# A decoder layer on eight cores: the second half's out projection from a bf16 copy of its weights, its normalisation with factors in PSUM, and four smaller moves around them

## The chip, the cores and the metric

The kernel runs on all 8 cores of one Trainium2 chip: two dies, cores 0 to 3 and 4 to 7. Each core does its own share of the tokens, and the time is the device time of the slowest core in microseconds (us). PE is the matmul engine, DVE the vector engine, ACT the scalar engine, POOL (GpSimd) the fourth compute engine, and SP an engine that does nothing here but issue DMAs. SBUF and PSUM are on-chip memories; PSUM is what matmuls write to, used here as 8 banks.

Some executions of these 8-core versions show a lower clock and the time is some per cent longer (3459.4 us once for the kernel before). Only fast runs are compared here. A profile names source lines of its own kernel, so one operation has another line number before and after; the text gives both.

## The reference, cut to what matters

One layer: a projection, two kinds of attention, an RMS norm for each group of heads, the out projection, a LayerNorm, a SwiGLU feed-forward block, a second LayerNorm.

```python
y = jnp.concatenate([rms_norm(ya, g_mix_a), rms_norm(yb, g_mix_b)], axis=-1)   # (tokens, 2048)
mix = jnp.einsum('bse,ed->bsd', y, w_out)                                      # out projection
x = layer_norm(ALPHA * x + mix, ln1_g, ln1_b)
x = layer_norm(ALPHA * x + swiglu(x, w_up, w_down), ln2_g, ln2_b)
```

The change touches the end of the attention, the RMS norm of y, the out projection and the sums of the first LayerNorm.

## The kernel before

A core has 2048 tokens. The out projection is made in two halves of 1024 tokens (`st` 0 and 1). A half has 32 tiles, one for each block `n` of 128 output columns and each group `hh` of 512 tokens. In the first half the first six tiles are half done early, while attention ends. For a tile, PE does 16 matmuls into one PSUM bank, DVE makes z = alpha * x + bank (which frees the bank and one of four x buffers), ACT squares z, and GpSimd adds z and its square to running sums. SP loads x.

```python
for si, (n, hh) in enumerate(steps):
    bk = OUT_BK[si % 6] if st == 0 else si % 4      # 6 banks in the first half, 4 in the second
    load_xr(si + 3)                                 # x of the third tile from here, on SP
    if st == 0 and si < 8:                          # the second half's y, 2 loads per tile, on SP
        for c in (KCB + KCA[:7])[2 * si:2 * si + 2]:
            k.y_load(1, c)
    ...                                             # out_mm: the matmuls of the tile
    if hh == 1:
        wdone(k, ("o", st, n))                      # frees the weights' slot and issues the next load
    for _ in range(2):                              # first half: normalise the second half's y
        if st == 0 and si >= 8 and k.norms:
            out_norm(k, *k.norms.pop(0))
    if si >= 1 and fins:
        fins.pop(0)()                               # LayerNorm sums of the half before, on PE
    ...                                             # DVE: z = alpha * x + bank
    ...                                             # stats(): ACT squares z, GpSimd sums z and z*z
    # ... then LayerNorm tiles of the half before, if due
```

The weights of a block `n` (512 KB in bf16) go through a ring of five slots. The loads cast from float32 and are issued by GpSimd, in the same queue of instructions as GpSimd's sums:

```python
def wfill(k):
    while k.wlist:
        key, src, n, a, p = k.wlist[0]
        if any(lo < p + n * 2 and p < hi for (_, lo, hi) in k.wlive):
            return
        ...
        if key[:2] == ("d", 1):
            k.S.dma("sp", v, src, [k.bwdb[key[2]]], [b], "ws")
        else:
            k.S.dma("pool", v, src, [], [b], "ws")

def out_norm(k, st, c, hh):          # y = y * gain * factor, on DVE, two inputs in SBUF
    r, br = k.rs[st * 2 + hh + (0 if c >= 8 else 4)]
    ...
    k.S.dve(lambda: nc.vector.scalar_tensor_tensor(out=v, in0=v, scalar=k.gmix[:, c:c + 1], in1=r, ...), [b, br, k.bsmall], [b])

def rs_load(k, rsum):                # the factors, on ACT's queue
    for t in range(4):
        k.S.dma("act", k.rs[t][0], k.rb_d[:, t * 512:(t + 1) * 512], [rsum[t]], [k.rs[t][1]], "rs")
```

Waits between engines are semaphores that the kernel's helper derives from what each operation reads and writes. In the traces an engine takes its instructions in order, and one that waits holds back all behind it; that includes the issue of a DMA.

The softmax here doesn't subtract the row's maximum and nothing guards it: scores larger than these inputs give would overflow.

## Time and profile before

Median 3056.03 us in the first three runs (3055.99 to 3057.72). The profiled execution was a further one, of 3060.24 us. Its page, taken on the slowest core (7): busy time of each engine with its share of the span, and the shares of the chain of waits that ended last.

```profile
PE 2987.2 (98%) x15999; PEld 1427.6 (47%) x15999; DVE 1063.9 (35%) x1442; ACT 656.1 (21%) x906; POOL 624.0 (20%) x591
...
PE 87%; DMA 5%; DVE 3%; issue 2%; ACT 2%; POOL 1%; ACTq 0%; SPq 0%; DVEq 0%; POOLq 0%
```

PE is busy 98% of the span. What is left to win by moving other work is in the gaps between matmuls, and in the clock: after or within four of PE's stops on this core the clock records show 0.5 for 3.4 to 10.2 us, and in these stretches a matmul of 128x512 starts every 427 ns, at full clock every 216 (medians). The groups of instructions show whose gaps those are. Columns: line, engine, operation, output<-input, shapes and count; busy us and mean ns of one; idle time of the engine just before them, with what ended it. L1135 is the out projection, L1375 the up projection after it, L1124 `out_norm`.

```profile
L1375 PE MATMUL sp<-arena 128*128 128x512 bf16 x5632 | 1219.0, 380 | 10.2 <-DVE arena L1271 10.2
...
L1135 PE MATMUL sp<-arena 128*128 128x512 bf16 x1024 | 233.3, 391 | 3.0 <-DVE arena L1271 2.3 <-DVE arena L1124 0.6
...
L1124 DVE SCALAR_TENSOR_TENSOR arena<-arena 128x512 bf16<-128x512 bf16 x64 | 76.6, 1237 | 4.3 <-ACT arena L966 4.3
```

The out projection hardly waits (3.0 us). The up projection waits once, 10.2 us, for L1271, which makes z. The waits of SP's queue say why these z are late: the last x loads reuse z slots, and SP stands until the stores of x1 out of these slots have landed (waited for: us in total, times, longest).

```profile
SPq L183 <- DMA x1s<-arena: 28.3, 4, 13.7
```

Stages are compared by windows. Columns: window, its length, busy us of PE, PEld (weight load), DVE, ACT and POOL with counts, granted clock, share of DMA time in use, GB/s. The first two windows are the first half of the out projection, 1060 to 1180 the second, 1180 to 1225 the start of the up projection.

```profile
968.00:1020.00 52.00, 51.93 (x235) 23.12 (x234) 31.57 (x29) 7.69 (x13) 37.09 (x32) 0.97 0.92 203
1020.00:1060.00 40.00, 37.67 (x174) 16.45 (x172) 33.72 (x29) 7.22 (x12) 34.66 (x30) 1.00 0.78 146
1060.00:1125.00 65.00, 61.83 (x255) 26.88 (x254) 36.22 (x55) 27.93 (x42) 46.66 (x45) 0.91 0.91 176
1125.00:1180.00 55.00, 55.00 (x234) 23.87 (x233) 30.53 (x47) 21.11 (x30) 36.32 (x33) 0.91 0.96 219
1180.00:1225.00 45.00, 34.81 (x151) 15.14 (x150) 4.76 (x7) 6.87 (x10) 16.97 (x16) 0.89 0.67 127
```

PE loses 10 of 45 us in 1180 to 1225. DMA is near full in the second half. Last, the timeline of the attention's tail. Columns: start, duration, engine, line, operation, output<-input, count, and in brackets the idle time before and what ended it.

```profile
893.22 2.15 ACTq L127 DMA_DIRECT2D arena<-rb  x4
...
895.47 0.60 ACT L925 ACTIVATE arena<-sp 128x512 f32<-128x512 f32 x1 [3.44 <-issue]
...
897.73 0.61 PE L897 MATMUL sp<-arena 128*128 128x128 bf16 x8 [1.95 <-DVE arena L928]
...
908.03 0.75 DVE L331 SCALAR_TENSOR_TENSOR arena<-sp,arena 128x512 f32<-128x512 f32 x1
...
908.89 1.02 DVE L334 TENSOR_TENSOR arena<-arena 128x512 bf16<-128x512 f32 x1
...
910.65 0.82 PE L908 MATMUL sp<-arena 128*128 128x64 bf16 x17 [2.14 <-DVE arena L700]
```

ACT issues the four factor loads for 2.15 us, so the activation behind them starts after 3.44 us of idle, and PE stops for 1.95 us. Later two operations of the rope (the rotation of queries and keys by position) stand on DVE ahead of a mask (L700), and PE stops for 2.14 us.

**A bookkeeping of stops.** I summed, from the trace, the gaps in which no matmul runs and half of the time at clock 0.5 (cold clock, in what follows), by stretch. I call the sum the loss. Not every stop has cold clock after it: the one near 700 was 1.92 us long on all 8 cores before, and 3.4 us at 0.5 followed it on cores 3, 4, 6 and 7 alone. A gap and a stretch of cold clock count where they begin. Where the clock is already at 0.5 while PE still stands, both are counted, so the loss runs somewhat high: without this overlap the whole of 640 to 1225 is 40.7 before. Where a reading turns on it, the text says so. The mean of the 8 cores for the kernel before, in us: 3.6 in 690 to 720, 13.7 in 880 to 943 (the tail), 2.3 in 968 to 1020, 2.1 in 1020 to 1060, 4.7 in 1060 to 1125, 8.2 in 1125 to 1225; with the little between them, 42.1 in 640 to 1225. Time lost at a third clock, 0.81, is kept apart (0.1875 of its length, for the records have 0.8125 there, and matmuls of 128x512 start every 263 ns; 6.8 us here).

### The profile page before, as it was taken

The numbers are of one execution on the slowest core, as the hardware profiler recorded it, in microseconds if no ns is written. First come the engines' busy times: TensorE is split into PE (matmuls) and PEld (weight loads), VectorE is DVE, ScalarE is ACT, GpSimd is POOL, SyncE is SP. The second block draws the span as 40 slices with busy tenths as digits, with TensorE's granted clock in tenths as the row PEclk, the third lists the DMA queues.
The fourth block names the chain that finished last, engine by engine and source line by source line (L and its number), as shares of the span: only waits on it lengthen the run. The fifth ranks groups of instructions, "written<-read, shape, count | busy, mean of one in ns | idle before, by whom it ended". The sixth has DMA issues, their size and how long they took to land.

```text
span 3059.1 us, 40208 instructions; the slowest of 8 cores (3041.8 to 3059.1 us)
## 1 busy us (share of the span) xinstructions
PE 2987.2 (98%) x15999; PEld 1427.6 (47%) x15999; DVE 1063.9 (35%) x1442; ACT 656.1 (21%) x906; POOL 624.0 (20%) x591
## 2 busy tenths in 40 slices
PE   8999999999999998999999999999999999999997
PEld 3445554556664443444444444444444444444443
DVE  1655546887785862430000100000222100000142
ACT  0000002765654142320000001111222000011222
POOL 2000001553444864000000002222000000002233
PEclk9999999999999998999999999999999999999998
DMA  9961213245668898564434348889666434434574
GB/s 166 183 146 54 83 48 76 56 120 136 150 148 176 163 179 175 127 129 75 80 72 83 70 95 204 206 206 200 144 153 137 86 71 82 72 109 180 177 234 149
DMA packets 192956, 397.92 MB, mean 130 GB/s; under 512 B 88961, under 2 KB 106625, under 8 KB 171778
## 3 DMA queue, kind: packets, MB, share of 16 engines
q0 software_dynamic: 31296, 167.06, 32.7%
q1 hardware_dynamic: 144194, 196.81, 21.6%
q10 hardware_dynamic: 17280, 31.46, 2.9%
q8 instruction: 129, 2.11, 0.3%
q14 instruction: 57, 0.47, 0.1%
HBM read 470.52 MB, written 91.82 MB: 184 GB/s over the span
## 4 chain that ended last, share of the span: by engine, by line
PE 87%; DMA 5%; DVE 3%; issue 2%; ACT 2%; POOL 1%; ACTq 0%; SPq 0%; DVEq 0%; POOLq 0%
PE sp L1375 40%; PE sp L1408 20%; PE sp L487 7%; PE sp L474 6%; PE sp L737 5%; DMA arena<-xres 3%; DMA arena<-wv 1%; PE sp L555 1%; DVE arena L1124 1%; PE sp L908 1%; DMA x1s<-arena 1%; PE sp L1135 1%; DVE arena L928 1%; PE sp L796 1%; ACT arena L926 1%
## 5 line engine op out<-in xcount | busy, mean ns | idle before, releaser
L1375 PE MATMUL sp<-arena 128*128 128x512 bf16 x5632 | 1219.0, 380 | 10.2 <-DVE arena L1271 10.2
L1375 PEld LDWEIGHTS sp<-arena 128*128 128x128 bf16 x5632 | 551.6, 98 | 678.1 <-issue 16.2
L1408 PE MATMUL sp<-arena 128*128 128x512 bf16 x2816 | 608.3, 379 | 0.0
L1383 DVE TENSOR_TENSOR arena<-sp,arena 128x512 bf16<-128x512 f32 x176 | 121.8, 692 | 998.6 <-ACT arena L1382 998.6
L1408 PEld LDWEIGHTS sp<-arena 128*128 128x128 bf16 x2816 | 275.5, 98 | 332.6 <-issue 0.6
L1382 ACT ACTIVATE arena<-sp 128x512 f32<-128x512 f32 x176 | 105.2, 598 | 903.8 <-PE sp L1375 903.8
L127 POOL DMA_DIRECT2D arena<-wup x88 | 46.8, 532 | 1086.0 <-PE sp L1375 1069.9
L1175 POOL TENSOR_TENSOR arena<-arena 128x512 f32<-128x512 f32 x119 | 156.1, 1312 | 458.3 <-DVE arena L1419 404.8
L1135 PE MATMUL sp<-arena 128*128 128x512 bf16 x1024 | 233.3, 391 | 3.0 <-DVE arena L1271 2.3
L737 PE MATMUL sp<-arena 128*128 128x512 bf16 x1024 | 235.5, 379 | 0.0
L1419 DVE SCALAR_TENSOR_TENSOR arena<-arena,sp 128x512 f32<-128x512 f32 x64 | 44.0, 688 | 518.9 <-PE sp L1408 279.9
L487 PE MATMUL sp<-arena 128*128 128x512 bf16 x1024 | 222.2, 379 | 0.0
L474 PE MATMUL sp<-arena 128*128 128x384 bf16 (+1 forms) x1040 | 182.6, 337 | 0.0
L1135 PEld LDWEIGHTS sp<-arena 128*128 128x128 bf16 x1024 | 102.0, 100 | 134.9 <-issue 42.0
L1176 POOL TENSOR_TENSOR arena<-arena 128x512 f32<-128x512 f32 x119 | 157.5, 1323 | 10.5 <-ACT arena L1174 10.5
L487 PEld LDWEIGHTS sp<-arena 128*128 128x128 bf16 x1024 | 100.2, 98 | 120.3
L700 DVE TENSOR_TENSOR arena<-arena 128x1024 bf16<-128x1024 bf16 x160 | 144.4, 916 | 21.0 <-ACT arena L871 10.6
L737 PEld LDWEIGHTS sp<-arena 128*128 128x128 bf16 x1024 | 96.6, 98 | 108.4 <-issue 1.6
L474 PEld LDWEIGHTS sp<-arena 128*128 128x128 bf16 x1040 | 101.7, 98 | 79.6
L346 ACT ACTIVATE arena<-sp,arena 128x512 bf16<-128x512 f32 (+1 forms) x37 | 25.2, 680 | 497.2 <-PE sp L511 383.0
L1403 ACT ACTIVATE arena<-arena 128x512 f32<-128x512 f32 x64 | 52.2, 816 | 354.3 <-DMA arena<-x1s 353.8
L1174 ACT ACTIVATE arena<-arena 128x512 f32<-128x512 f32 x119 | 75.1, 631 | 243.7 <-DVE arena L1419 100.2
(130 smaller groups left out, 2071.2 us busy)
## 6 DMA issues: line engine op xcount, KB each, us to landing
arena<-wup POOLq DMA_DIRECT2D x88, 1024.0 KB, 8.2
arena<-wdb SPq DMA_DIRECT2D x32, 1408.0 KB, 6.3
arena<-wdn POOLq DMA_DIRECT2D x16, 1408.0 KB, 13.2
wdb<-arena SPq DMA_DIRECT2D x16, 1408.0 KB, 12.7
arena<-wout POOLq DMA_DIRECT2D x32, 512.0 KB, 10.9
arena<-xres SPq DMA_DIRECT2D x64, 256.0 KB, 8.5
x1s<-arena ACTq DMA_DIRECT2D x64, 256.0 KB, 7.9
arena<-x1s SPq DMA_DIRECT2D x64, 256.0 KB, 6.5
```

The lines of the kernel that those rows point to most:

```text
L474: ins = nc.tensor.matmul(bank(k, bk)[:, 0:c1 - c0], x[:, kc, blk * 128:blk * 128 + 128], wv[:, kc, c0:c1], start=(kc == 0), stop=(kc == KC ...
L487: ins = nc.tensor.matmul(bank(k, bk), wk[h][:, kc, :], x[:, kc, :], start=(kc == 0), stop=(kc == KC - 1))
L700: S_.dve(lambda: nc.vector.tensor_tensor(out=pg, in0=pg, in1=m.to_broadcast([128, rows, 1024 // rows]), op=ALU.mult), [bp, b], [bp])
L737: ins = nc.tensor.matmul(bank(k, bk), w[:, kc, :], x[:, kc, :], start=(kc == 0), stop=(kc == KC - 1))
L1135: ins = nc.tensor.matmul(bank(k, bk), w[:, kc, :], y[:, kc, hh * 512:(hh + 1) * 512], start=(first and i == 0), stop=(last and i == len(kc ...
L1174: S_.act(lambda: nc.scalar.activation(out=sq, in_=z, func=AF.Square), [bz], [bsq])
L1175: S_.pool(lambda: nc.gpsimd.tensor_tensor(out=za, in0=za, in1=z, op=ALU.add), [bz, bza], [bza])
L1176: S_.pool(lambda: nc.gpsimd.tensor_tensor(out=qa, in0=qa, in1=sq, op=ALU.add), [bsq, bqa], [bqa])
L1375: ins = nc.tensor.matmul(bank(k, a + half), w[:, kc, half * 128:half * 128 + 128], xb[:, kc, hh * 512:(hh + 1) * 512], start=(kc == 0), st ...
L1382: S_.act(lambda si=si, a=a: nc.scalar.activation(out=sg[si][0], in_=bank(k, a), func=AF.Silu), [k.bBK[a]], [sg[si][1]])
L1383: S_.dve(lambda si=si, a=a, f=f, hh=hh: nc.vector.tensor_tensor(out=h[f][:, hh * 512:(hh + 1) * 512], in0=bank(k, a + 1), in1=sg[si][0], o ...
L1408: ins = nc.tensor.matmul(bank(k, bk), w[:, fc, :], h[fc][:, hh * 512:(hh + 1) * 512], start=(fc == 0), stop=(fc == FC - 1))
```

## The change

It has six parts. (1) In the first half SP stores each weight block out of its slot, already bf16, and in the second half SP loads it back, instead of a second cast load on GpSimd. (2) The second half's `out_norm` reads its factor from PSUM, where ACT copies it; this takes banks 4 to 7, so the first half turns over 4 banks from tile 6 on, not 6. (3) The LayerNorm sums on PE come one tile later. (4) The factor loads move from ACT's queue to GpSimd's. (5) A flush of queued rope work on DVE at the attention's tail is taken out. (6) `reduce_b(3)` near 700 us moves into the next step. The intent: fewer DMA bytes in the second half, faster normalisation on DVE, and no PE stops at the five places where it stopped.

```diff
@@ attention
         if u == 26:
-            run(dveq, 9)
             for i in KCA[:6]:
                 k.y_load(0, i)
...
+            if u == 1 and p_ == 1:
+                reduce_b(3)
...
-        if u == 0:
-            reduce_b(3)
@@ def rs_load(k, rsum):
-        k.S.dma("act", k.rs[t][0], ...
+        k.S.dma("pool", k.rs[t][0], ...
@@ the list of weights, and wfill
-        k.wlist += [(("o", st, n), k.wout_d[n], ...
+        k.wlist += [(("o", st, n), (k.wout_d, k.wob_d)[st][n], ...
...
+        elif key[:2] == ("o", 1):
+            k.S.dma("sp", v, src, [k.bwob[key[2]]], [b], "ws")
@@ def out_norm(k, st, c, hh):
+    if st == 1:
+        i = 4 + hh + (0 if c >= 8 else 2)
+        if c in (0, 8):
+            k.S.act(lambda r=r: nc.scalar.activation(out=bank(k, i), in_=r, func=AF.Copy), [br], [k.bBK[i]])
+        r, br = bank(k, i), k.bBK[i]
@@ the loop over out tiles
-            bk = OUT_BK[si % 6] if st == 0 else si % 4
+            bk = OUT_BK[si] if st == 0 and si < 6 else (si + 2 - 2 * st) % 4
...
+            if st == 0 and hh == 0:
+                w, bw = k.wts[("o", 0, n)]
+                S_.dma("sp", k.wob_d[n], w, [bw], [k.bwob[n]], "wob")
             if hh == 1:
                 wdone(k, ("o", st, n))
...
-            if si >= 1 and fins:
+            if si >= 2 and fins:
                 fins.pop(0)()
```

More of the change, by code (lines that the diff above doesn't have):

```diff
@@ L239, in build @@
     k.wdb_d = dt("wdb", [KC, 128, FC, 128], BF16, kind="Internal").ap()
+    k.wob_d = dt("wob", [KC, 128, KC, 128], BF16, kind="Internal").ap()
     k.x1s_d = dt("x1s", [KC, 128, TOK], F32, kind="Internal").ap()
@@ L1080, in out_open @@
     k.wlist = []
+    k.bwob = [Buf("wob%d" % n) for n in range(KC)]
     for st in range(2):
-        k.wlist += [(("o", st, n), k.wout_d[n], KC * 128, KC, (n + 16 * st) % 5 * 4096) for n in range(KC)]
+        k.wlist += [(("o", st, n), (k.wout_d, k.wob_d)[st][n], KC * 128, KC, (n + 16 * st) % 5 * 4096) for n in range(KC)]
     for st in range(2):
@@ L1094, in rs_load @@
     for t in range(4):
-        k.S.dma("act", k.rs[t][0], k.rb_d[:, t * 512:(t + 1) * 512], [rsum[t]], [k.rs[t][1]], "rs")
+        k.S.dma("pool", k.rs[t][0], k.rb_d[:, t * 512:(t + 1) * 512], [rsum[t]], [k.rs[t][1]], "rs")
 def wfill(k):
```

## The prediction

> **What bounds it now.** The page has the PE 98% busy (2987 of 3059 us); the chain of waits is 87% PE. The change touches the tail of the attention and the two out projections (880 to 1200 us) and one place near 700, so some 1% is at stake. PE stops between 640 and 1245 us on core 7, the slowest (from the trace's instructions):
>
> - 700: 1.92 us, for the DVE eviction behind reduce_b(3)'s two activations; then 3.4 us at clock 0.5.
> - 896: 1.95 us. In the timeline the ACT queue issues four factor loads for 2.15 us; the activation behind them is 3.4 late.
> - 908.5: 2.14 us. The flush of rope work puts three operations ahead of a mask; then 6.8 us at 0.5.
> - 1069: 3.17 us. LN's sums wait for GpSimd (1.31 + 1.32 us per tile); then 3.4 us at 0.5.
> - 1189: 10.19 us before the up projection, waiting for the last z, which wait for x loads (chain: a 22 us x1 store, a 10.9 us x load); then 10.2 us at 0.5.
>
> [...] Half of each is lost.
>
> **Second half's normalisation.** These 32 operations take 0.74, 1.75, 1.16, 3.11 us in turn; with GpSimd idle (953 to 963) 0.74. [...] DVE is full from 1000 to 1040 and makes a z every 3.82 us, where PE needs 3.46. With the factor in PSUM I expect 0.7 us each, like the evictions with one PSUM input (0.68). Four activations of 0.6 us are added. Gain about 4 us.
>
> **DMA.** A cast load of an out weight is 128 packets of about 410 ns, 3.3 us of all 16 engines; a bf16 load from SP, by packets of 4 KB now at 172 ns, 1.4 us. The first half gets 16 stores of some 1.3 us: it carries 10 us more, the second half 20 less of 110 at 95% busy. I expect the stop at 1189 to shrink from 10 us to 2 to 5, with its cold clock.
>
> **What costs.** From tile 6 the first half turns over 4 banks, not 6. On all cores z of tile 8 comes late (986 to 998 us: x load 22 us to landing, behind the y loads); PE starts tile 12 at about 990. With 4 banks tile 12 needs that z: a new stop of 5 to 8 us, cold clock 2 to 3, lengthened by two or three weight stores in SP's queue. This eats the normalisation's gain and more.
>
> **Sum, core 7:** 700: -2.5; 896: -2; 908: -5; LN sums: -4.9; normalisation: -4; banks: +9; end: -8: about -17. On core 4 (3053 us, no stop at 1189, 13.7 us lost to clock 0.81) the gain is nearer 8; it may become the slowest. [...]
>
> **Predicted:** 3041 us, 3028 to 3056 in 8 of 10. Faster by over 2%: 0.01; within 2%: 0.97; slower: 0.02.
>
> **Right or wrong shows in:** norms at 0.7 us; no stop at 700, 896, 908, 1069; a new stop near 985 to 998 waiting for z; second-half out weights landing in under 7 us (10.9 now); DMA share in the second half below 0.9; a shorter stop before the up projection.
>
> **What would make it wrong:** weight loads or stores blocking x loads in SP's queue; the moved reduce_b(3) or the GpSimd factor loads making new stops; the 0.81 clock taking back what is won.

The sum came to -2.5 - 2 - 5 - 4.9 - 4 + 9 - 8 = -17.4 us. "Half of each" is half of each stretch at clock 0.5 (matmuls started every 427 ns there, every 216 at full clock). That the factor in PSUM would make the normalisations fast was an estimate, from their 0.74 us with GpSimd idle, up to 3.11 with it busy, and the 0.68 of the evictions with one PSUM input.

## The result, and the profile after

| | median us | fast runs, lowest to highest |
|---|---|---|
| before | 3056.88 (4 runs, one of them slow; 3056.03 without it) | 3055.99 to 3057.72 |
| after | 3049.51 (4 runs) | 3047.5 to 3051.08 |

The ratio of the fast runs is 0.9977 (95% interval 0.9957 to 0.9996): some 7 us shorter where 15 were predicted. Here and below a ratio is the mean time of one kernel's fast runs over that of the other's in the same rounds, so it is not quite the ratio of the medians quoted. All outputs are right.

The page of after is that of core 1, now the slowest; all that follows it is core 7 again, as before. The chain's share of DMA is 9%, where core 7 had 5% before.

```profile
PE 2974.6 (98%) x15999; PEld 1423.2 (47%) x15999; DVE 1034.2 (34%) x1442; ACT 657.8 (22%) x910; POOL 612.4 (20%) x579
...
PE 82%; DMA 9%; DVE 3%; ACT 2%; issue 2%; SPq 1%; POOL 1%; DVEq 0%; ACTq 0%; POOLq 0%
```

The groups of core 7 (L1144 out projection, L1387 up projection, L1133 `out_norm`, in two forms since half of them read PSUM):

```profile
L1387 PE MATMUL sp<-arena 128*128 128x512 bf16 x5632 | 1216.6, 379 | 0.0
...
L1144 PE MATMUL sp<-arena 128*128 128x512 bf16 x1024 | 228.7, 385 | 19.7 <-DVE arena L1283 19.0 <-DVE arena L1133 0.6
...
L1133 DVE SCALAR_TENSOR_TENSOR arena<-arena 128x512 bf16<-128x512 bf16 x32 | 25.5, 840 | 4.6 <-ACT arena L967 4.6
...
L1133 DVE SCALAR_TENSOR_TENSOR arena<-arena,sp 128x512 bf16<-128x512 bf16 x32 | 22.4, 742 | 24.3 <-ACT sp L1130 24.3
```

The wait before the up projection is gone (10.2 to 0.0). The normalisations with the factor in PSUM take 742 ns, as predicted. But the out projection now waits 19.7 us for z (L1283), and the normalisations wait 24.3 us for the copies of their factors (L1130). The same windows as before:

```profile
968.00:1020.00 52.00, 39.22 (x164) 16.58 (x163) 17.74 (x27) 6.65 (x11) 27.63 (x26) 0.90 0.97 232
1020.00:1060.00 40.00, 39.42 (x183) 17.76 (x182) 17.65 (x27) 8.54 (x14) 32.28 (x30) 1.00 0.98 231
1060.00:1125.00 65.00, 59.32 (x259) 26.09 (x257) 30.03 (x46) 23.43 (x36) 36.84 (x31) 0.97 0.64 199
1125.00:1180.00 55.00, 55.00 (x257) 24.95 (x255) 37.44 (x58) 26.67 (x37) 42.10 (x35) 1.00 0.93 260
1180.00:1225.00 45.00, 45.00 (x206) 20.33 (x205) 7.50 (x11) 7.51 (x11) 14.66 (x14) 1.00 0.54 103
```

968 to 1020 has lost 13 us of PE, where DMA has little room (0.97) and DVE, POOL and ACT are all less busy than before (DVE in part because its normalisations are shorter). That picture, everyone less busy at once, is one of engines standing in line behind something. The waits of core 7 name it (first three: compute engines and POOL's DMA issues; last two: SP's queue):

```profile
POOL arena L127 <- DMA wob<-arena: 30.6, 6, 10.0
...
DVE arena L1133 <- ACT sp L1130: 24.3, 4, 9.0
...
PE sp L1144 <- DVE arena L1283: 19.0, 6, 7.8
```

```profile
SPq L183 <- DMA wob<-arena: 28.3, 5, 6.0
...
SPq L183 <- DMA x1s<-arena: 6.3, 4, 2.5
```

`wob<-arena` is the new store of a weight block. GpSimd waits 30.6 us for such stores to land, SP 28.3 us. The old wait for the x1 stores has shrunk from 28.3 to 6.3 us, with fewer bytes to read in the second half (the core's reads from memory over the whole run: 470.5 MB before, 462.1 after). The timeline of core 7 shows how a wait of GpSimd for a store reaches PE:

```profile
983.05 0.57 POOL L127 DMA_DIRECT2D arena<-wout  x1 [8.55 <-DMA wob<-arena]
...
984.30 0.69 DVE L1283 SCALAR_TENSOR_TENSOR arena<-arena,sp 128x512 f32<-128x512 f32 x1 [10.49 <-DMA arena<-xres]
...
998.54 0.57 POOL L127 DMA_DIRECT2D arena<-wout  x1 [9.97 <-DMA wob<-arena]
...
1001.72 0.63 ACT L1183 ACTIVATE arena<-arena 128x512 f32<-128x512 f32 x1 [10.97 <-POOL arena L1185]
...
1010.92 1.41 DVE L1133 SCALAR_TENSOR_TENSOR arena<-arena,sp 128x512 bf16<-128x512 bf16 x2 [8.45 <-ACT sp L1130]
```

PE's own timeline, with the two stops that follow:

```profile
985.34 4.94 PE L1144 MATMUL sp<-arena 128*128 128x512 bf16 x13 [7.77 <-DVE arena L1283]
```

```profile
1013.18 3.10 PE L1144 MATMUL sp<-arena 128*128 128x512 bf16 x7 [4.99 <-DVE arena L1283]
```

The stop of 7.77 us comes from an x load that stood on SP behind y loads and stores (10.49). It takes the four banks as well. In the kernel before, the z of the next tile came as late on core 7, with y loads but no stores ahead of its x load on SP:

```profile
985.44 0.69 DVE L1271 SCALAR_TENSOR_TENSOR arena<-arena,sp 128x512 f32<-128x512 f32 x1 [9.65 <-DMA arena<-xres]
```

There PE had six banks, and did not stop. The stop of 4.99 us is a chain of five engines. A weight slot is freed one tile (3.5 us) after its store was issued, but the store lands 10.1 us after issue (median of core 7). The load into that slot, on GpSimd, waits 9.97 us for the store. GpSimd's sums stand behind it; ACT's square waits for them (10.97), having one buffer for squares; the copy of a factor stands behind the squares on ACT; the normalisation waits for the copy (8.45); and z, which would free a bank, stands behind the normalisation on DVE. With the two stops the clock records of core 7 show 0.5 for 6.8 us (from 982.5 on, before the first stop ends) and for 3.4 us.

In the second half the same store is met again, from SP. These lines are of core 7's timeline:

```profile
1076.46 0.38 SPq L127 DMA_DIRECT2D wob<-arena  x1
...
1082.94 0.32 SPq L127 DMA_DIRECT2D arena<-wob  x1
1083.35 6.86 SPq L127 DMA_DIRECT2D arena<-xres  x5
...
1089.12 0.69 DVE L1283 SCALAR_TENSOR_TENSOR arena<-arena,sp 128x512 f32<-128x512 f32 x1 [13.66 <-DMA arena<-xres]
...
1108.08 4.14 PE L1144 MATMUL sp<-arena 128*128 128x512 bf16 x11 [4.04 <-DVE arena L1283]
```

SP issues the last store at 1076.46, then stands until 1082.94 for the slot and its load; five x loads wait behind, z is 13.66 us late, and a while later PE stops for 4.04 us. (That the one led to the other is tested below.)

The tail of the attention has a new stop where the old ones were:

```profile
908.90 0.75 DVE L1133 SCALAR_TENSOR_TENSOR arena<-arena 128x512 bf16<-128x512 bf16 x1
909.57 0.69 DVE L929 TENSOR_TENSOR arena<-sp,arena 128x512 bf16<-128x512 f32 x1
...
910.40 0.61 PE L898 MATMUL sp<-arena 128*128 128x128 bf16 x8 [4.35 <-DVE arena L929]
```

PE waits 4.35 us for the DVE eviction L929, which stands behind ropes, masks and normalisations.

Summed by the bookkeeping, the loss (mean of 8 cores, us):

| stretch | before | after |
|---|---|---|
| 690 to 720 | 3.6 | 1.4 |
| 880 to 943, tail of attention | 13.7 | 13.0 |
| 968 to 1020, first half | 2.3 | 17.2 |
| 1020 to 1060, first half | 2.1 | 0.5 |
| 1060 to 1125, second half | 4.7 | 5.4 |
| 1125 to 1225, its end and the up projection | 8.2 | 0.1 |
| 640 to 1225 in all | 42.1 | 44.8 |
| lost at clock 0.81, 640 to 1225 | 6.8 | 0.0 |

So stops and cold clock did not shrink at all on average: what the change won at the end (8.1 us) and near 700 (2.2) it lost in 968 to 1020 (14.9). That these two profiled runs differ by 5.5 us in the mean span (3050.5 to 3045.0) is mostly the 0.81 clock, 6.8 us in one and none in the other, against which the loss rose by 2.7. It was back in a later run of the same changed kernel (7.6 us, run e9 below), so the change does not do away with it.

### The profile page after: what moved, and what is told of

The parts are those of the page before. It is cut to its first block, busy times and chain, and to the rows that moved or that the text cites. A ratio compares the mean times of both kernels' runs of the same rounds, so it can differ in the third digit from the quotient of the medians.

```text
span 3048.4 us, 40274 instructions; the slowest of 8 cores (3038.6 to 3048.4 us)
## 1 busy us (share of the span) xinstructions
PE 2974.6 (98%) x15999; PEld 1423.2 (47%) x15999; DVE 1034.2 (34%) x1442; ACT 657.8 (22%) x910; POOL 612.4 (20%) x579
## 4 chain that ended last, share of the span: by engine, by line
PE 82%; DMA 9%; DVE 3%; ACT 2%; issue 2%; SPq 1%; POOL 1%; DVEq 0%; ACTq 0%; POOLq 0%
PE sp L1387 40%; PE sp L1420 12%; PE sp L488 7%; PE sp L475 6%; PE sp L738 5%; DMA arena<-x1s 5%; PE sp L1144 3%; DMA wob<-arena 2%; SPq L127 1%; DMA arena<-wv 1%; PE sp L556 1%; PE sp L909 1%; DVE arena L929 1%; ACT arena L1415 1%; ACT arena L926 1%
## 5 line engine op out<-in xcount | busy, mean ns | idle before, releaser
L1387 PE MATMUL sp<-arena 128*128 128x512 bf16 x5632 | 1216.6, 379 | 0.0
L1387 PEld LDWEIGHTS sp<-arena 128*128 128x128 bf16 x5632 | 551.0, 98 | 665.9 <-issue 2.6
L1144 PE MATMUL sp<-arena 128*128 128x512 bf16 x1024 | 227.5, 383 | 19.0 <-DVE arena L1283 18.3
L1184 POOL TENSOR_TENSOR arena<-arena 128x512 f32<-128x512 f32 x119 | 152.7, 1283 | 426.6 <-DVE arena L1431 402.1
L1144 PEld LDWEIGHTS sp<-arena 128*128 128x128 bf16 x1024 | 100.3, 99 | 146.4 <-issue 31.5
L1185 POOL TENSOR_TENSOR arena<-arena 128x512 f32<-128x512 f32 x119 | 153.5, 1290 | 4.6 <-ACT arena L1183 4.6
L1415 ACT ACTIVATE arena<-arena 128x512 f32<-128x512 f32 x64 | 52.1, 814 | 357.6 <-DMA arena<-x1s 357.0
```

Of the source, the lines that this page charges most:

```text
L1144: ins = nc.tensor.matmul(bank(k, bk), w[:, kc, :], y[:, kc, hh * 512:(hh + 1) * 512], start=(first and i == 0), stop=(last and i == len(kc ...
L1184: S_.pool(lambda: nc.gpsimd.tensor_tensor(out=za, in0=za, in1=z, op=ALU.add), [bz, bza], [bza])
L1185: S_.pool(lambda: nc.gpsimd.tensor_tensor(out=qa, in0=qa, in1=sq, op=ALU.add), [bsq, bqa], [bqa])
L1387: ins = nc.tensor.matmul(bank(k, a + half), w[:, kc, half * 128:half * 128 + 128], xb[:, kc, hh * 512:(hh + 1) * 512], start=(kc == 0), st ...
L1415: S_.act(lambda xb=xb, n=n: nc.scalar.activation(out=xb, in_=xb, func=AF.Identity, bias=k.lnp[:, 1, n:n + 1], scale=k.lnp[:, 0, n:n + 1]), ...
```

## The experiments

Fourteen more runs were made, on four chips (e9 is the change once more); each ratio is against the kernel before on the same chip. The questions: which part of the change makes the new loss in 968 to 1020 (the stores, the y loads ahead of the x loads, or the four banks), what the other parts are worth, and what is left when the loss is taken away. The edits are against the kernel after unless said.

The texts name theories by letters. A: the weight copy's stores make the loss; A1, its later and sharper form: by holding weight slots, for which GpSimd and SP then stand. B: the turn over four banks makes it. C: the y loads ahead of the x loads in SP's queue make it. D: in the attention's tail DVE is full, and edits there only move stops.

| run | ratio of fast runs (95%) | 880–943 | 968–1020 | 1060–1125 | 1125–1225 | 640–1225 |
|---|---|---|---|---|---|---|
| after, first run | 0.9977 (0.9957–0.9996) | 13.0 | 17.2 | 5.4 | 0.1 | 44.8 |
| e9, after again | 0.9971 (0.9946–0.9997) | 13.1 | 16.1 | 4.3 | 1.2 | 43.9 |
| e1, no weight copy | 0.997 (0.9953–0.9988) | 13.7 | 9.6 | 1.5 | 17.1 | 50.3 |
| e2, before + 4 banks | 0.9978 (0.9959–0.9996) | 14.4 | 7.2 | 0.1 | 11.3 | 46.9 |
| e3, before + copy | 0.9981 (0.9955–1.0007) | 14.1 | 15.0 | 8.7 | 0.9 | 51.4 |
| e4, six banks | 0.9989 (0.9942–1.0036) | 13.9 | 17.6 | 11.4 | 0.4 | 52.7 |
| e5, stores earlier | 0.9955 (0.9932–0.9977) | 13.1 | 10.6 | 0.4 | 1.1 | 34.3 |
| e6, y loads earlier | 0.9954 (0.9929–0.9979) | 13.2 | 5.5 | 7.2 | 0.1 | 35.7 |
| e7, flush back | one look | 13.4 | 18.6 | 5.4 | 0.1 | 46.5 |
| e8, factor loads on ACT | one look | 15.7 | 17.6 | 6.4 | 0.2 | 49.0 |
| e10, e5 and e6 | 0.9956 (0.9912–0.9999) | 13.1 | 7.3 | 0.4 | 0.1 | 29.7 |
| e11, e10 + six banks | 0.9916 (0.989–0.9943) | 13.1 | 5.9 | 1.0 | 3.1 | 32.3 |
| e12, e10 + norms later | 0.9929 (0.9902–0.9955) | 13.2 | 6.2 | 0.4 | 0.8 | 29.4 |
| e13, e10, factor in SBUF | one look | 13.0 | 9.0 | 1.0 | 2.0 | 35.4 |
| e14, e10, LN sums back | one look | 13.6 | 8.3 | 0.1 | 0.2 | 31.0 |

The columns of loss are the mean of the 8 cores in the one profiled run. Two runs of the same kernel, after and e9, agree within 1.1 us in each stretch, which is the size below which I read nothing. The times say less than these columns, since the slowest of 8 cores decides them and the runs of the kernel before spread over 20 us on the chip of e9 (3053.67 to 3074.31).

### e1_no_copy: the change without the weight copy

```diff
-        k.wlist += [(("o", st, n), (k.wout_d, k.wob_d)[st][n], ...
+        k.wlist += [(("o", st, n), k.wout_d[n], ...
-        elif key[:2] == ("o", 1):
-            k.S.dma("sp", v, src, [k.bwob[key[2]]], [b], "ws")
-            if st == 0 and hh == 0:
-                w, bw = k.wts[("o", 0, n)]
-                S_.dma("sp", k.wob_d[n], w, [bw], [k.bwob[n]], "wob")
```

> The kernel after without the bf16 weight copy (no stores, second half's weights cast from float32 on GpSimd as before). Theory A (the stores give the gain back: they hold weight slots, so that GpSimd's and SP's queues wait, 33 and 28 us in the profile after): the PE stops between 970 and 1020 us fall from 11 to 13 us a core to under 4, the stop before the up projection comes back with 3 to 10 us on some cores; time 0.995 to 0.999 of before. Theory B (the turn of 4 banks makes the stops): the stop near 976 to 990 stays at 5 us or more, and with the end stop back the time is 1.000 to 1.004 of before.

Measured: median 3059.48 us; the loss in 968 to 1020 falls from 17.2 to 9.6, that in 1060 to 1125 from 5.4 to 1.5, and the end of the second half loses 17.1 us (8.2 in the kernel before). The theory that blames the stores expected under 4 in the first stretch, and missed; its rival expected a stop of 5 us or more near 976 to 990 to stay, and one was there on six of the cores, of 5.07 to 7.34 us for z, at 983 to 993. That is the place and the length that the prediction gave the stop of the four banks, and no weight store is left in this kernel. So the stores account for some 7 us of the 15, and there is a second cause. And without the copy the stop at the end is back, so the copy is what takes it away (e3 shows the same from the other side). In the whole of 640 to 1225 the copy as written still gains 5.5 us of loss (50.3 without it, 44.8 with it), or 2.2 with the overlap of stops and cold clock taken out.

### e2_banks4: the kernel before, with four banks in the first half

```diff
-            bk = OUT_BK[si % 6] if st == 0 else si % 4
+            bk = OUT_BK[si] if st == 0 and si < 6 else (si + 2 - 2 * st) % 4
```

> The kernel before with nothing changed but the banks of the first half (4 in turn from tile 6 on). Theory B, as in the prediction: a new stop of 5 to 8 us near 985 to 998 on most cores, 5 to 10 us slower than before (1.002 to 1.003). Theory A: stops of less than 3 us there, within 3 us of before.

Measured: median 3062.11 us. The loss in 968 to 1020 rises by 4.9 us (2.3 to 7.2): the banks cost something, but less than their theory said, for it wanted a stop of 5 to 8 us on most cores and one core (6) had a wait of that length for z, of 5.50 us. The time did not follow: the ratio to the kernel before is 0.9978. The stop for the LayerNorm sums at 1069 had vanished (4.7 to 0.1 us in that stretch). The waits of core 7 show where the banks cost:

```profile
PE sp L1135 <- DVE arena L1271: 6.8, 9, 3.0
```

Nine short waits for z, the longest 3.0 us: on this core four banks alone do not make the stop of 7.77 us. With the change's other parts, and without the copy, they come near it (e1, up to 7.34).

### e3_copy_only: the kernel before, with the weight copy alone

The edit is the copy's part of the change (store, list of weights, SP branch).

> The kernel before with only the bf16 copy (stores in the first half, loads on SP in the second). Theory A: GpSimd waits some 30 us for the stores and SP some 25, new PE stops of 5 to 10 us between 970 and 1110; the stop before the up projection goes; net within 4 us of before. Theory B: no new stop over 3 us in the first half, 8 to 14 us faster than before (0.9955 to 0.9975).

Measured: median 3064.54 us, ratio 0.9981. With six banks and none of the other edits, the loss in 968 to 1020 is 15.0 us and in 1060 to 1125 it is 8.7; at the end 0.9. So the copy as written makes the new loss without the four banks. But PE waits for something else, too:

```profile
PE sp L1139 <- DMA arena<-wout: 9.0, 2, 7.5
```

With two more banks PE runs further ahead of z, and then meets the late weights: GpSimd issues their loads late, having stood 25.9 us for stores.

### e4_six_banks: the change with six banks

Two factor banks are used in turn, so six stay for the tiles.

```diff
-        i = 4 + hh + (0 if c >= 8 else 2)
+        i = 4 + (0 if c >= 8 else 1)
-            bk = OUT_BK[si] if st == 0 and si < 6 else (si + 2 - 2 * st) % 4
+            bk = OUT_BK[si % 6] if st == 0 else si % 4
```

> The kernel after with the factors in two banks (4 and 5, each written again for the second 512 tokens), so that the first half turns over 6 banks as before. Theory B: the stops near 976 and 1010 fall to under 3 us and the kernel is 7 to 12 us faster than the one after (0.994 to 0.9955 of before). Theory A: they shrink by less than half, under 4 us faster than after.

Measured: median 3059.83 us; the loss is 17.6 us in 968 to 1020, as with four (17.2). My prediction had put the new loss under the name of the banks; giving the banks back does nothing for the sum. The waits of core 7:

```profile
POOL arena L127 <- DMA wob<-arena: 38.8, 8, 17.7
...
PE sp L1144 <- DMA arena<-wout: 13.9, 5, 8.3
PE sp L1144 <- DVE arena L1283: 13.0, 3, 9.0
```

The loss moved. The first stop, 4.2 to 7.9 us at 972 to 987 in the change, is now 2.7 us at most, so it did need the four banks; but PE, further ahead, then waits 7.9 to 11.8 us for weights at 1000 to 1017 on seven cores. Those loads stand on GpSimd behind stores that land late.

### e5_store_early: each store two blocks earlier

The store of a block is issued long before the slot is freed, so that nothing waits for it; bytes and banks stay as in the change.

```diff
-            if st == 0 and hh == 0:
-                w, bw = k.wts[("o", 0, n)]
-                S_.dma("sp", k.wob_d[n], w, [bw], [k.bwob[n]], "wob")
+            if st == 0:
+                for m in range(5) if si == 0 else [n + 2] if hh == 1 and 3 <= n < 14 else []:
+                    w, bw = k.wts[("o", 0, m)]
+                    S_.dma("sp", k.wob_d[m], w, [bw], [k.bwob[m]], "wob")
```

> The kernel after with the same weight stores earlier: five at once before the first of the out tiles, then each four tiles before its weight slot is freed. Bytes and places of everything else are unchanged. Theory A1 (queues wait for the stores that hold weight slots): GpSimd's and SP's waits for the stores, 31 and 28 us on core 7 of the kernel after, fall under 6 us each; stops with cold clock between 968 and 1020 (mean of cores 17 us after) fall to some 8, those between 1060 and 1125 (5.4) under 2; 7 to 12 us faster than the kernel after. Theory A2 (the bytes of the stores crowd the DMA engines): the stops keep two thirds or more of their length, within 4 us of the kernel after.

Measured: median 3046.15 us, ratio 0.9955. Core 7's waits for stores:

```profile
POOL arena L127 <- DMA wob<-arena: 1.2, 1, 1.2
```

```profile
SPq L183 <- DMA wob<-arena: 1.2, 2, 0.8
```

They were 30.6 and 28.3 us. The loss in 968 to 1020 falls to 10.6, and that in 1060 to 1125 from 5.4 to 0.4, so the stop at 1104 did come from SP's wait for its last store. By the ratios, taken on different chips, it is some 5 to 7 us faster than the change. A1 had expected some 8 in the first stretch and 7 to 12 us faster, so it was right in kind and somewhat too bold; A2, the bytes, expected two thirds of the loss or more to stay, and 10.6 of 17.2 is just under that. The bytes are the same as in the change, so what went (6.6 us and 5.0) was the held slots. That the bytes are free is not shown: on six cores PE now waits 2.1 to 5.7 us for weights at 976 to 985, where the kernel without the copy (e1) waits 1.7 us at most for weights.

### e6_y_early: the second half's y loads issued at the first tile

```diff
-            if st == 0 and si < 8:
-                for c in (KCB + KCA[:7])[2 * si:2 * si + 2]:
+            if st == 0 and si == 0:
+                for c in KCB + KCA[:7]:
                     k.y_load(1, c)
```

> The kernel after with all 15 loads of the second half's y issued at the first out tile, where the DMA engines are half idle (943 to 960), not two per tile. Theory C (the y loads crowd the x loads of tiles 7 to 9): stops with cold clock between 968 and 1020 fall from 17 us to under 10, with the waits of GpSimd and SP for the stores little changed. Theory A1: they stay over 12, for the weight slots are held as before.

Measured: median 3048.1 us, ratio 0.9954. The loss in 968 to 1020 falls to 5.5, while the stores still hold up GpSimd (24.4 us) and SP (27.9 us), and 1060 to 1125 keeps its 7.2. So the second cause is the x loads that come late behind the y loads in SP's queue. It is one stop with the four banks, not a third cause: the kernel before has the x load as late on core 7 (9.65 us) and, with six banks, no stop there; e1 has the stop with no weight store in the queue. (The change without copy and with six banks, which would close this, was not run.) The two cures overlap: e5 takes away 6.6 us of the stretch and e6 11.7, and both together (e10) leave 7.3. They do not add up.

### e7_flush_back and e8_loads_act: two parts of the attention's tail undone

```diff
         if u == 26:
+            run(dveq, 9)
```

> The kernel after with the flush of the rope queue put back. Theory of the prediction: the stops with cold clock between 880 and 943 grow by about 5 us (12.9 in the mean of cores now). Rival D (DVE is full in this stretch, and the flush only orders its work): they change by less than 1.5 us.

Measured: 13.4 us of loss in 880 to 943 against 13.0; one look, 3053.59 us. That is under the 1.5 us of the rival's forecast: taking the flush out gained nothing that this shows. I had put it at 5 us.

```diff
-        k.S.dma("pool", k.rs[t][0], ...
+        k.S.dma("act", k.rs[t][0], ...
```

> The kernel after with the factor loads back on the ACT queue. Theory of the prediction: stops with cold clock between 880 and 943 grow by 2 us or more, with a stop of about 2 us near 892 to 896 again. Rival: the stops shift within the stretch, its sum changes by less than 1 us.

Measured: 15.7 us against 13.0, with the stop of 2.2 to 3.35 us at 891 to 894 back; one look, 3056.97 us. So the factor loads on GpSimd are worth 2.7 us.

### e9_after_again: the change once more, as a control

> The kernel after, unchanged, as the control on the chip of the next three. All theories: 0.996 to 0.999 of before; stops with cold clock near 17 us between 968 and 1020 and 5 us between 1060 and 1125, none before the up projection.

Measured: median 3057.03 us on this chip, ratio 0.9971. The means of its fast runs and of the kernel before's are 3057.5 and 3064.1 us for the slowest core, but 3049.2 and 3050.9 for the mean of the 8 cores: most of the gain of the change is in the slowest core. In the profiled run the 0.81 clock took 7.6 us in the mean of cores, all of it on cores 2 and 3, in one stretch of 161.8 us on each (their mean clock over the run is 0.986 and 0.984, that of the others 0.993 to 0.995).

### e10_both_early: e5 and e6 together

> The kernel after with the weight stores early and all y loads at the first out tile. If the two causes add (stores holding weight slots; y loads crowding x loads): stops with cold clock between 968 and 1020 under 5 us (10.6 with the stores early alone, 5.6 with the y loads early alone), under 1 us between 1060 and 1125; 0.993 to 0.995 of before. If the two compete for the half idle stretch before 960: 8 us or more remain, no faster than either alone.

Measured: median 3043.82 us, ratio 0.9956; two of its six fast runs, 3064.8 and 3071.8 us, had cores at a clock of 0.984 to 0.986, which widens the interval. The loss in 640 to 1225 is 29.7 us, the table's lowest but e12. In 968 to 1020 it is 7.3, neither under 5 nor 8 or more, so neither forecast held cleanly; and e6 alone had left 5.5 there. What remains is one stop at 970 to 974 on four of the cores (6.7, 7.2, 8.5, 8.6 us), in which z waits 14.3 to 16.2 us for an x load: now 15 y loads and five stores are issued in one burst ahead of it.

### e11_both_six: e10 with six banks

The edit is that of e4, made to e10.

> The kernel with both early, and the first half back on 6 banks with the factors in two. Theory B (the turn of 4 banks costs, as the prediction had it, once the stores no longer make the weights late): the stops left between 968 and 1020 fall by half or more, up to 5 us faster than with both early. Rival: what is left waits for weights or x loads, within 1.5 us of it.

Measured: median 3040.85 us, ratio 0.9916 (0.989 to 0.9943). This is the best version here, below both kernels; on the same chip the change itself had 0.9971. In 968 to 1020 the loss is 5.9 against 7.3, so two banks are worth 1.4 us there, close to what two runs of one kernel differ by. The longest stop is now one for weights, on core 6:

```profile
PE sp L1144 <- DMA arena<-wout: 7.8, 1, 7.8
```

By the bookkeeping e11 (32.3) is no better than e10 (29.7), so I do not claim that the banks are what made it faster in time; the mean of all cores' fast runs is 3030.4 us against e10's 3036.7, and 3032.3 without e10's two runs at the lower clock. The rival's forecast, that what is left waits for weights or x loads and the banks give less than 1.5 us, is the one that held.

### e12_norms_later: e10 with the tail's normalisations moved two steps later

```diff
-NORM_AT = ... ((25, (1, 2)), (26, (0, 1, 2)), (27, (0, 1, 2)), (28, (0, 2)), (29, (0, 2)), (30, (0, 2)), (31, (0, 2)))
+NORM_AT = ... ((25, (1, 2)), (27, (0, 1, 2)), (28, (0, 1, 2)), (29, (0, 1, 2)), (30, (0, 1, 2)), (31, (0, 2)))
```

> The kernel with both early, and the three normalisations of unit 26 of the attention, where the last rope work is, put into units 28 to 30. Theory D (DVE is full in unit 26): the stop of 4 us near 905 to 908 falls under 2 us on most cores, and the sum of stops with cold clock between 880 and 943 from 12.9 to 9 or less; 3 to 5 us faster than with both early. Rival (the stop follows the late factor loads or the ropes alone): the sum changes by less than 1.5 us.

Measured: median 3045.07 us, ratio 0.9929. The stop near 905 falls from 4.0–4.4 us, on five cores of e10, to about 2 us, but the loss in 880 to 943 stays (13.2 against 13.1): the stops came later. Theory D had forecast 9 or less for the sum, and missed; the rival's forecast of a change under 1.5 us held. With e7 this shows that these changes of order move stops about and leave the sum. That the load of DVE is why (54.79 of 63 us busy in the change, by the windows) is argued, not shown: no run took work from DVE there.

### e13_norm_sbuf and e14_ln_back: two parts of the change undone in e10

```diff
-    if st == 1:
+    if False:
```

> The kernel with both early, its second half's normalisation reading the factors from SBUF again (the banks stay). If the prediction's term is right (DVE held up by GpSimd costs PE about 4 us), stops between 1020 and 1060 grow from 0.2 us to 2 to 5 in the mean of cores and the 32 operations take up to 3.1 us again. Rival (PE does not feel it): stops grow by less than 1 us.

Measured: one look, 3048.4 us. The normalisations go back to the times of before. The group on core 7:

```profile
L1133 DVE SCALAR_TENSOR_TENSOR arena<-arena 128x512 bf16<-128x512 bf16 x64 | 84.4, 1359 | 7.3 <-ACT arena L967 4.6 <-DMA arena<-rb 2.6
```

The durations of the second half's 32 sum to 57.7 us, one of 7.12 that I did not follow and the others up to 3.12 us, against 23.7 in e10 (52.1 in the kernel before). Yet PE loses only 1.5 us more in 1020 to 1060 (1.7 against 0.2), less than the 2 to 5 I expected and more than its rival's under 1. So 34 us of DVE time were worth 1 to 2 us of PE time there, with four banks. The whole of 640 to 1225 loses 5.7 us more (35.4 against 29.7), but the rest is in single stops: 1.7 in one that begins at 968 to 970, before the second half's normalisations do, and most of what follows 1060 on two cores alone. Whether it belongs to the normalisations one look cannot say.

```diff
-            if si >= 2 and fins:
+            if si >= 1 and fins:
```

> The kernel with both early, its LN sums one tile earlier, as in the kernel before. If the later sums are what removed the stop near 1069 (3.2 us there, 4.7 us with cold clock in the mean of cores between 1060 and 1125), a stop of 2 us or more comes back on most cores. Rival (GpSimd is no longer behind, as its operations no longer meet DVE's): less than 1 us comes back.

Measured: one look; of three runs only the profiled one was fast, 3042.57 us. The loss in 1060 to 1125 stays at 0.1: the later sums bought nothing here. Something else took the stop at 1069 away. It had gone in e2, too, where PE came to it some 5 us later; that PE's delay is the reason here, and not the rival's (GpSimd no longer behind), is not shown.

## Why the prediction was right or wrong

The prediction was wrong in size: 15 us shorter was forecast, 7 measured. Its sum for core 7 against the trace of core 7, stops and cold clock, us:

| term of the prediction | predicted | measured on core 7 |
|---|---|---|
| "700: -2.5" | -2.5 | -3.0 |
| "896: -2; 908: -5" | -7 | -2.8 (880 to 943) |
| "LN sums: -4.9; normalisation: -4" | -8.9 | +0.8 (1020 to 1125: -1.7 and +2.5) |
| "banks: +9" | +9 | +17.8 (968 to 1020) |
| "end: -8" | -8 | -15.3 (1125 to 1225) |
| sum | "about -17" | -2.5 from these; the whole of 640 to 1225: -2.7 |
| clock 0.81, not in the sum | – | -10.6, in this pair of runs |

**The step that failed is "banks: +9".** It was mis-sized by a factor of two, for it held one mechanism of two. The one that it had was right in kind: four banks and an x load late behind the y loads make a stop for z ("a new stop near 985 to 998"; it came at 977 to 985, of 7.77 us and 3.4 of cold clock, and in e1, without any weight store, at 983 to 993). What it had wrong is the cost of the stores. I wrote that they would lengthen this stop as "two or three weight stores in SP's queue": I counted them as bytes in a queue. In the runs they make a stop of their own, the chain that starts on GpSimd (4.99 us and 1.7 of cold clock on core 7, and the weights that come late in e3 and e4). So the banks were not the lever that the term made of them: four banks alone cost 4.9 us (e2), the loss is the same with six (e4), and the copy alone makes 15.0 with six (e3). A store reads its weight slot, so the next load into that slot waits until it has landed. In the change it was issued 3.5 us before the slot was freed and landed in about 10, so GpSimd stood 30.6 us and SP 28.3 us, each with other work behind the waiting issue. With the store early enough these waits are 1.2 us each, and the loss falls with the bytes unchanged (e5). The prediction did list "weight loads or stores blocking x loads in SP's queue" under what would make it wrong; that was part of it, and the block on GpSimd, through the sums and the squares to DVE, was not on the list. The end of the second half missed the other way (-15.3 for -8), so two wrong terms partly hid each other in the sum; that is luck.

**"908: -5" failed for another reason.** The flush was ahead of the mask at 908, but taking it out did not take work from DVE. On core 7 DVE was busy 53.87 us of 880 to 943 before and 54.79 after; the ropes came elsewhere, and PE stopped for the eviction at 906 instead. Undoing the edit changes nothing (13.4 against 13.0, e7), and moving the normalisations away changes nothing in the sum either (e12). In a stretch in which one engine is so busy, a stop could not be costed by what stood before it. The part at 896 was right in size: the GpSimd factor loads are worth 2.7 us (e8).

**The normalisation was right by itself, and little of it is seen in PE's time.** On core 7 of the kernel before, normalisations (both inputs in SBUF) and GpSimd's instructions took longer in most places where they overlapped: a normalisation took 0.73 to 0.75 us alone and 0.74 to 3.12 beside GpSimd, and GpSimd's two sums took 1.64 and 1.71 us beside a normalisation, 1.27 and 1.26 otherwise (medians). With the factor in PSUM a normalisation took 0.740 to 0.748 us throughout. By what mechanism is not shown. But in 1020 to 1060, where DVE had been full, the change gained 1.6 us of PE time in the mean of cores (2.1 to 0.5), not 4, and e13 against e10 gives 1.5; and the 24.3 us that the normalisations waited for ACT's copies are a link of the second stop. "LN sums: -4.9": the stop at 1069 went, and with it that loss, but e14 shows that it stays away without the edit, once the other parts are in; and the stop at 1104, from SP's wait, took its place in the change.

**Right:** 700; the normalisations at 0.7 us; the end of the second half, where the stop of 10 us went altogether rather than to 2 to 5. The copy does this: without it the end loses 17.1 us (e1), with it alone 0.9 (e3). That a plain bf16 load from SP is cheaper here than a cast load from GpSimd held: the median from issue to landing went from 10.9 to 5.7 us on core 7, and to 7.3 on core 1, so "under 7" held on the one and not on the other. What made it cheaper is not shown, for the load has another issuer and no cast, reads half the bytes (bf16 for float32), and stands beside fewer others. The DMA share of the second half went below 0.9 only in its first part (0.64, then 0.93).

**The 0.81 clock** was named as a risk, and was larger than the change: 6.8 us lost on average in the profiled run of the kernel before, none in that of the change, 7.6 again in e9. In the first it came in stretches of 3.5 to 25.3 us, at nearly the same times on the two cores of a pair (2 and 3, 4 and 5, 6 and 7); cores 0 and 1 had none. In all fast runs the mean clock of a core was 0.982 to 0.997. What the time shows as a gain of 7 us is in most part the slowest core's; the mean core gained 1.7 us on the chip of e9.

**What stays open.** Why the 0.81 clock comes in some fast runs and not in others, and why the stop near 700 was followed by clock 0.5 on four cores and not on the other four. How much of the 7.3 us that e10 still loses in 968 to 1020 is the burst of y loads and stores ahead of the x load, and how much the banks: I tried the banks (1.4 us), not another order of the burst. Whether the bytes of the stores cost anything once they are early (e5). Why, in the attention's tail, the loss stays whatever the order. And whether e11 is faster than e10 at all: without e10's two runs at the lower clock the mean cores differ by 1.9 us.

## What to carry to other kernels

A store that reads a buffer holds it as a computation does: issue it so early that it has landed before the next writer of that buffer is issued, for a DMA issue that waited held back everything behind it on its engine, sums and x loads included (GpSimd stood 30.6 us and SP 28.3 us here, and 1.2 us each with the stores earlier). When a DMA is added, cost what it holds (slot, queue order, the issuer's time) and not its bytes only. And in a stretch in which an engine is nearly full (DVE, 54.79 of 63 us), two changes of order moved the stops and did not shrink their sum; taking work away from it was not tried here.
